# State-space stage, merge and dt of a hybrid decoder block: rooms in another order, dt's chain elsewhere, exponents without a mask product

## The chip, the cores and the metric

The kernel runs on one core of a Trainium2 chip. The metric is the time of one execution in device microseconds (us), as the median of several runs. A profiled execution gives the trace: what each engine did and when, in us from the start of its span. The engines are TensorE (PE, matmuls; PEld is its loading of weights), VectorE (DVE), ScalarE (ACT), GpSimd (POOL) and SyncE (SP), which here issues the transfers between the chip's memory and the working memory (DMA).

## The reference

One layer of a hybrid decoder block on a sequence of 1024 tokens of width 1024, in float32. After a norm, one input projection gives the queries, keys and values of a stick-breaking attention with 16 heads, the z, x, B, C and dt of a Mamba-2 state-space mixer with 32 heads in 4 groups, and two gates per channel. Both branches are projected to the width, gated and summed, and go through an output projection; then come a cross-attention into 256 memory tokens and a feed-forward part. The lines that matter here are those of the mixer:

```
dt = softplus(dt_raw + dt_bias);  a = -exp(a_log)
a_cs = cumsum(dt * a)                       # within each chunk of 128
decay = exp(where(tril, a_cs[l] - a_cs[s], -inf))
cb = einsum('bclgn,bcsgn->bcgls', C, B)
y_diag = einsum('bcgls,bcgels,bcsgep->bclgep', cb, decay, x * dt)
states = einsum('bclgn,bcgel,bclgep->bcgepn', B, exp(a_cs[-1] - a_cs), x * dt)
```

The mask `tril` keeps, in each 128 x 128 square of a chunk, the pairs in which the source is not later than the target.

## The kernel before, in words

Matmuls of float32 values are made as three products of two-part values: a higher part (a copy in the matmul's own format, mostly by ACT, helper line L94) and a lower part (the difference, mostly by DVE, helper line L97). L100, L101 and L102 are these three products. The order of the work on each engine is not written out: a scheduler with a model of the engines sets it when the program is built, from the order in the source, the dependences and the rooms (the named buffers of each pool). Pools are placed one after the other in the working memory, so that a pool's place in the source also decides whose earlier room it takes over, and which earlier work it must wait for.

The stages that matter here, with their times in the trace of before:

- **z stage, to about 270 us.** `token_major` makes a pair of column blocks of v or z from seven (or, with two made early, five) block products of 48 matmuls each, in a scheme that saves one product in eight. Each product's steps split a piece of the weights (L94 by ACT, L97 `zl<-zr,zh` by DVE, three rooms) and make 12 matmuls. The pieces come in by `zr` loads. Sums of products are made in rooms named "zk", six in all (L542, L545, L550).
- **Conv stage, about 270 to 700 us.** x, B and C are made in pairs of row blocks (`winograd_pair`, L218 to L239), convolved on DVE (L602) and transposed. `dt_chain` (L633 to L678) runs inside it, ahead of the seventh pair: it loads the raw dt, laid out as 128 rows of 256, computes softplus by a series (L647 to L660), the sum along each chunk by a scan (L666), and the logarithm of dt (L670), and writes the sums and keys in two parts to the scratch arrays `sum_d` and `key_d` (L674 to L678). `dt_columns`, two pairs later, takes dt and the sums from `dts`.
- **Attention**, to about 1102 us.
- **State-space stage, about 1102 to 1500 us.** 32 chunks (4 groups of 8). `open_four` prepares B, C and cb (L995, L997) for four chunks. `prep` makes the exponents of a chunk as a matmul of two arrays of rows: `keyrows` (keys, and two rows of ones) and `colrows` (a pattern of ones, and the sums), 512 columns at a time (L1021). Ahead of it, a product of the identity and `bar` (L1020) puts the mask, -2^120 above the diagonal, into the same accumulator. ACT takes the exponential (L1022), DVE multiplies by cb (L1023). Then come the states (pst), the outputs (po, and the 16 small matmuls pd, L1073), the norm and the `flip` (four transposes, L1095), and the projection of the branch. Beside the first chunks, `memory` norms and transposes the 256 memory tokens (L1147 to L1154) and the K and V products of the cross-attention are made from them (`mm<-oth,bw` with 256 columns first). Raw weights ("wraw") and split weights ("bw") share the pool "w3".
- **Merge, from about 1500 us.** The attention's output is loaded from `o_d` and split (L1309, "m2" rooms), multiplied by the attention branch's weights (`both`, L1296, one block f of 128 columns ahead), gated and added; the weights of the output projection (`w_mix_out`, L1277) come in meanwhile.

All DMA issues named here stand in SP's one queue, in order.

Of the kernel before, what the change touches and what calls it, by code (L numbers as in the profile page):

```python
# [8 lines left out]
F32 = mybir.dt.float32  # L9
F32R = mybir.dt.float32r  # L10
# [6 lines left out]
P = 128  # L17
# [13 lines left out]
FILL_LEFT, FILL_RIGHT = 96, 224  # L31


@with_exitstack
def hybrid_block(ctx, tc, a, out, dbg=None):
# [44 lines left out]
    u_d = scr("u_d", [4, P, HALF])  # L80

# [167 lines left out]
    with ExitStack() as pa:  # L249
# [214 lines left out]
        with ExitStack() as p1:  # L464
# [24 lines left out]
            def token_major(j, c0, put, i0, early=False):  # L489
# [10 lines left out]
                def times(*args):  # L500
                    for f in product(*args):
                        f()

# [53 lines left out]
            token_major(1, C_Z, put_z, 0, True)  # L557
# [11 lines left out]
        with ExitStack() as p1:  # L569
# [63 lines left out]
            def dt_chain():  # L633
                aneg = mk(cp, [P, 1], F32, "aneg")
                for q in range(4):
                    nc.sync.dma_start(aneg[q * 32:(q + 1) * 32], a["a_log"][0].unsqueeze(1))
                A.activation(aneg, aneg, AF.Exp)

                QT = S // 4
                da, db = [mk(t4, [P, S], F32, "b4") for _ in range(2)]  # L640
                u, e, rc, q_ = [da[:, i * QT:(i + 1) * QT] for i in range(4)]
                keep = db[:, 0:QT]
                dtb = mk(cp, [P, 1], F32, "dtb")
                for q in range(4):
                    nc.sync.dma_start(u[q * 32:(q + 1) * 32], dt_d[:, q * QT:(q + 1) * QT])
                    nc.sync.dma_start(dtb[q * 32:(q + 1) * 32], a["dt_bias"][0].unsqueeze(1))
                V.tensor_scalar(u, u, dtb, None, ALU.add)  # L647
                V.scalar_tensor_tensor(e, u, -1.0, u, ALU.mult, ALU.max)
                A.activation(e, e, AF.Exp, scale=-1.0)

                V.tensor_scalar(rc, e, 2.0, None, ALU.add)
                V.reciprocal(rc, rc)
                V.tensor_tensor(e, e, rc, ALU.mult)
                s2 = rc
                V.tensor_tensor(s2, e, e, ALU.mult)
                V.tensor_scalar(q_, s2, 1.0 / 17, None, ALU.mult)
                for i in range(7, 0, -1):
                    V.scalar_tensor_tensor(q_, q_, 1.0 / (2 * i + 1), s2, ALU.add, ALU.mult)
                V.scalar_tensor_tensor(q_, q_, 1.0, e, ALU.add, ALU.mult)
                V.tensor_scalar(q_, q_, 2.0, None, ALU.mult)  # L660
                dtf, adt, acs = dts[:, 0], e, dts[:, 1]
                V.scalar_tensor_tensor(dtf, u, 0.0, q_, ALU.max, ALU.add)
                V.tensor_scalar(adt, dtf, aneg, -1.0, ALU.mult, ALU.mult)
                G.memset(keep, 1.0)
                G.memset(keep.rearrange("h (c t) -> h c t", t=P)[:, :, 0:1], 0.0)
                V.tensor_tensor_scan(acs, keep, adt, 0.0, ALU.mult, ALU.add)  # L666

                key, ln = db[:, QT:2 * QT], db[:, 2 * QT:3 * QT]
                V.tensor_scalar(key, dtf, 1e-37, None, ALU.max)
                A.activation(ln, key, AF.Ln)  # L670
                V.tensor_tensor(key, ln, acs, ALU.subtract)
                for (src, dst), (hi, lo) in zip(((acs, sum_d), (key, key_d)), ((u, e), (rc, q_))):
                    hi, lo = hi.bitcast(F32R), lo.bitcast(F32R)
                    V.tensor_copy(hi, src)  # L674
                    lo_of(lo, src, hi)
                    for j, t in enumerate((hi, lo)):
                        for q in range(4):
# [1182 lines left out]
```

## Time and profile before

| | us |
|---|---|
| median of three runs (lowest, highest) | 2608.21 (2608.04, 2610.14) |
| the profiled execution | 2607.02 |
| its span | 2605.2 |
| PE busy | 2507.7 (96%) |
| DVE busy | 1826.8 (70%) |
| ACT busy | 1152.4 (44%) |
| POOL busy | 891.3 (34%) |
| mean granted TensorE clock | 0.991 of full speed |

Busy time is the time in which an engine has an instruction in hand. Matmuls are pipelined, so their recorded lengths overlap: 12090 matmuls are recorded. A row of the groups of instructions gives line, engine, operation, out<-in with shapes and count, then the busy time and the mean ns of one, then the idle time ahead of them and what ended it. A row of the waits gives who waited for whom, us in all, times, and the longest.

### The profile page before, as it was taken

How to read it: one execution, taken by the hardware profiler on the slowest of the kernel's cores; microseconds unless marked ns; L12 is line 12 of the kernel's file. 1: busy time of each engine (PE TensorE's matmuls, PEld its weight loads, DVE VectorE, ACT ScalarE, POOL GpSimd, SP SyncE). 2: the span in 40 equal slices, each digit the busy share in tenths (PEclk: the TensorE clock that was granted, in tenths of full speed). 3: DMA queues.
4: the chain of work that ended last, by engine and by line, in shares of the span. 5: the costliest groups of instructions: out<-in, count | busy, mean ns of one | idle time of the engine just before them, and what ended most of it. 6: DMA issues, size and time to landing. Idle time of an engine off the chain costs nothing. (4 is left out here: it accounts for less than half of the span.)

```text
span 2605.2 us, 32757 instructions
## 1 busy us (share of the span) xinstructions
PE 2507.7 (96%) x12090; PEld 2078.6 (80%) x12090; DVE 1826.8 (70%) x2111; ACT 1152.4 (44%) x2053; POOL 891.3 (34%) x686
## 2 busy tenths in 40 slices
PE   8999999999999999979999999999999999999998
PEld 6788787787787778777888878887787888888877
DVE  7675777776689898687788654415549566666997
ACT  6333455554466665455544312314333333334433
POOL 5330544443111111254555231100113333333675
PEclk9999999999999999999999999999999999999999
DMA  6441333333422322255332362221231223224322
GB/s 227 151 138 68 126 122 107 100 105 112 115 77 58 89 68 67 90 166 185 107 92 72 119 201 77 100 86 42 93 121 60 90 73 98 73 89 178 129 97 97
DMA packets 243755, 278.02 MB, mean 107 GB/s; under 512 B 14975, under 2 KB 171272, under 8 KB 243210
## 3 DMA queue, kind: packets, MB, share of 16 engines
q1 hardware_dynamic: 243594, 275.92, 33.4%
q8 instruction: 95, 1.56, 0.2%
q14 instruction: 66, 0.54, 0.1%
HBM read 197.61 MB, written 69.87 MB: 103 GB/s over the span
## 5 line engine op out<-in xcount | busy, mean ns | idle before, releaser
L834 DVE TENSOR_TENSOR_SCAN n<-n,mask 128x128 f32<-128x128 f32 (+7 forms) x128 | 180.2, 1432 | 10.4 <-ACT n L833 7.7
L97 DVE TENSOR_TENSOR sw<-sf,sw 128x512 fp32r<-128x512 f32 x150 | 128.2, 868 | 64.0 <-ACT sw L94 63.6
L194 POOL TENSOR_TENSOR sf<-wr,wr 128x512 f32<-128x512 f32 x38 | 57.1, 1504 | 290.9 <-DMA wr<-in_w_gu_dram 105.7
L853 ACT ACTIVATE wth<-tr,mone 128x512 fp32r<-128x512 f32 x192 | 111.1, 581 | 75.6 <-PE tr L850 74.0
L94 ACT ACTIVATE sw<-sf 128x512 fp32r<-128x512 f32 x150 | 91.8, 626 | 102.2 <-PE mm L220 90.4
L854 DVE SCALAR_TENSOR_TENSOR wtl<-tr,wth 128x512 fp32r<-128x512 f32 x192 | 101.6, 546 | 39.2 <-ACT wth L853 37.8
L97 DVE TENSOR_TENSOR sw<-wr,sw 128x512 fp32r<-128x512 f32 x113 | 107.8, 956 | 30.2 <-ACT sw L94 25.8
L94 ACT ACTIVATE sw<-wr 128x512 fp32r<-128x512 f32 x113 | 71.0, 629 | 127.9 <-PE mm L220 126.7
L220 PE MATMUL mm<-h,sw 128*128 128x512 f32 x320 | 125.0, 392 | 1.8 <-DVE sw L97 1.8
L218 PE MATMUL mm<-h,sw 128*128 128x512 f32 x320 | 122.6, 391 | 3.1 <-ACT h L94 2.3
L219 PE MATMUL mm<-h,sw 128*128 128x512 f32 x320 | 125.3, 391 | 0.0
L100 PE MATMUL mm<-oth,bw 128*128 128x512 f32 (+1 forms) x320 | 122.1, 381 | 0.3 <-ACT a L1130 0.3
L102 PE MATMUL mm<-oth,bw 128*128 128x512 f32 (+1 forms) x320 | 119.0, 372 | 0.3 <-DVE bw L97 0.3
L101 PE MATMUL mm<-otl,bw 128*128 128x512 f32 (+1 forms) x320 | 118.5, 370 | 0.0
L90 POOL TENSOR_SCALAR v<-va 128x512 fp32r<-128x512 f32 x16 | 20.7, 1296 | 279.1 <-PE av L863 148.7
L602 DVE SCALAR_TENSOR_TENSOR b<-b,prmT,b 128x1023 f32<-128x1023 f32 (+2 forms) x72 | 106.0, 1472 | 12.6 <-ACT b L600 12.1
L163 POOL TENSOR_SCALAR rstd<-ms 128x1 f32<-128x1 f32 x82 | 33.1, 404 | 233.5 <-ACT x L1352 112.6
L833 ACT ACTIVATE n<-sc 128x512 f32<-128x512 f32 (+1 forms) x192 | 89.2, 487 | 48.6 <-PE tr L850 23.1
L100 PE MATMUL p<-bw,h 128*128 128x512 f32 x256 | 98.6, 390 | 3.3 <-DVE x L1354 2.4
L97 DVE TENSOR_TENSOR zl<-zr,zh 128x512 fp32r<-128x512 f32 x84 | 72.7, 880 | 40.5 <-ACT zh L94 40.4
L196 POOL TENSOR_TENSOR sf<-wr 128x512 f32<-128x512 f32 x38 | 63.6, 1675 | 108.3 <-DVE sw L97 108.3
L102 PE MATMUL p<-bw,h 128*128 128x512 f32 x256 | 100.5, 393 | 0.1
(595 smaller groups left out, 8266.2 us busy)
## 6 DMA issues: line engine op xcount, KB each, us to landing
wr<-in_w_gu_dram SPq DMA_DIRECT2D x80, 256.0 KB
wr<-in_w_in_dram SPq DMA_DIRECT2D x36, 512.0 KB
zr<-in_w_in_dram SPq DMA_DIRECT2D x32, 512.0 KB
gu_d<-t SPq DMA_DIRECT2D x44, 256.0 KB
wraw<-in_w_in_dram SPq DMA_DIRECT2D x20, 512.0 KB
xs_d<-b SPq DMA_DIRECT2D x32, 256.0 KB
s<-xs_d SPq DMA_DIRECT2D x32, 256.0 KB
s<-zs_d SPq DMA_DIRECT2D x32, 256.0 KB
```

The lines of the kernel that those rows point to most:

```text
L94: A.activation(o, i, AF.Copy)
L97: eng.tensor_tensor(o, i, hi.bitcast(F32), ALU.subtract)
L100: first = T.matmul(ps, sh, mh, start=start, stop=False)
L101: T.matmul(ps, sh, ml, start=False, stop=False)
L102: T.matmul(ps, sl, mh, start=False, stop=stop)
L218: T.matmul(ps, w[0][:, k, :], b[0][:, k, :], start=first and k == 0, stop=False, skip_group_check=True)
L219: T.matmul(ps, w[0][:, k, :], b[1][:, k, :], start=False, stop=False, skip_group_check=True)
L220: T.matmul(ps, w[1][:, k, :], b[0][:, k, :], start=False, stop=last and k == 3, skip_group_check=True)
L602: V.scalar_tensor_tensor(acc[:, sh:], y[:, :S - sh], cw(3 - sh, f), acc[:, sh:], ALU.mult, ALU.add)
L834: V.tensor_tensor_scan(nt[:, 0:L][:, ::-1], nt[:, 0:L][:, ::-1], mask[:, S - L:][:, ::-1], 1.0, ALU.mult, ALU.max)
L853: A.activation(wh[:, t0 * P:], pt[:, t0 * P:], AF.Identity, bias=mone)
L854: V.scalar_tensor_tensor(wl[:, t0 * P:], pt[:, t0 * P:], -1.0, wh[:, t0 * P:].bitcast(F32), ALU.add, ALU.subtract)
```

## The change

Four things change. The mask of the exponents is no longer a product: `colrows` is filled with -2^120 in those rows (times the identity, so that each key row that isn't a head's or a one's picks out one column), `keyrows` holds ones above the diagonal in these rows, and so the one product L1021 also adds a large negative number to most masked places; what is left over is dealt with by a triangle on cb (an `affine_select` on POOL, per four chunks) and by cutting the exponential at 3e38 in the product with cb, which becomes a three-operand instruction. dt's chain becomes a generator whose pieces are issued between the steps of z's first pair; its rooms are four of the six "zk", and dt and its sums go through a new scratch array `dts_d`, from where the conv stage loads them at its start. The raw weights of the state-space stage get a pool of their own. In the merge, the pool of the branch's weights and their load come first in the source, and the loads of the attention's output take turns between two new rooms and four "m2" (six before).

```diff
+BIG, FAR = 3.0e38, -(2.0 ** 120)
...
+    dts_d = scr("dts_d", [2, P, S // 4])
...
+            def dt_chain():
+                QT = S // 4
+                aneg, dtb = [mk(cp, [P, 1], F32, n) for n in ("aneg", "dtb")]
+                rooms = [mk(kp, [P, HALF], F32, "zk") for _ in range(4)]
+                u, e, rc, q_, keep, key, ln, dtf = [t[:, i * QT:(i + 1) * QT] for t in rooms for i in range(2)]
...
+                for j, t in enumerate((dtf, acs)):
+                    nc.sync.dma_start(dts_d[j], t)
...
-            def token_major(j, c0, put, i0, early=False):
+            def token_major(j, c0, put, i0, early=False, beside=()):
+                beside = iter(beside)
...
                     for f in product(*args):
                         f()
+                        next(beside, None)
...
-            token_major(1, C_Z, put_z, 0, True)
+            token_major(1, C_Z, put_z, 0, True, dt_chain())
...
-            def dt_chain():
...
+            for j in range(2):
+                nc.sync.dma_start(dts[:, j], dts_d[j])
             for i, j in enumerate(order):
-                if i == 6:
-                    dt_chain()
...
+        wr = pool(p3, "w3raw", 3)
         wp = pool(p3, "w3", 2)
...
-        identr = mk(ep, [P, P], F32R, "identr")
-        V.tensor_copy(identr, ident)
-        bar = mk(ep, [P, 4, P], F32R, "bar")
-        tri = mk(t4, [P, GH, P], F32, "s4")
-        G.memset(tri, 0.0)
-        G.affine_select(tri, tri, [[0, GH], [1, P]], ALU.is_ge, -(2.0 ** 120), base=0, channel_multiplier=-1)
-        V.tensor_copy(bar, tri[:, 0:4, :])
...
-        for t in colrows + keyrows:
-            G.memset(t.bitcast(F32), 0.0)
         for t in colrows:
+            V.tensor_scalar(t, ident.unsqueeze(1).to_broadcast([P, GH, P]), FAR, None, ALU.mult)
+            for r, n in ((0, GH), (32, GH), (ONES, 2)):
+                V.tensor_scalar(t[:, :, r:r + n], ident[:, r + n:r + n + 1].unsqueeze(1).to_broadcast([P, GH, n]), FAR, None, ALU.mult)
...
+        u = mk(sm, [P, 4, P], F32, "cb")
+        G.memset(u, 1.0)
+        G.affine_select(u, u, [[0, 4], [1, P]], ALU.is_gt, 0.0, base=0, channel_multiplier=-1)
         for t in keyrows:
+            V.tensor_copy(t, u.rearrange("p c i -> p (c i)"))
...
             A.activation(cb, pm, AF.Copy)
+            G.affine_select(cb, cb, [[0, 4], [1, P]], ALU.is_ge, 0.0, base=0, channel_multiplier=-1)
...
-                T.matmul(pe, identr, bar, start=True, stop=False)
-                T.matmul(pe, f4["keys"][:, cs], cr[:, hs, :], start=False, stop=True)
+                T.matmul(pe, f4["keys"][:, cs], cr[:, hs, :], start=True, stop=True)
...
-            V.tensor_tensor(seg, seg, f4["cb"][:, ci, :].unsqueeze(1).to_broadcast([P, GH, P]), ALU.mult)
+            V.scalar_tensor_tensor(seg, seg, BIG, f4["cb"][:, ci, :].unsqueeze(1).to_broadcast([P, GH, P]), ALU.min, ALU.mult)
...
-            xt = mk(wp, [P, D], F32, "wraw", bufs=3)
+            xt = mk(wr, [P, D], F32, "wraw")
...
+        wp = pool(p4, "w4", 1)
+        ol_ = pool(p4, "oload", 2)
         op = pool(p4, "oatt")
-        t2 = pool(p4, "t2m", 6)
-        wp = pool(p4, "w4", 1)
+        t2 = pool(p4, "t2m", 4)
...
-                t = mk(t2, [P, HALF], F32, "m2")
+                t = mk(t2 if k % 2 else ol_, [P, HALF], F32, "m2")
```

The scheduler's order follows from this. At the opening of the state-space stage, PE before; `mm` with 256 columns is memory's K product, `ptr` a flip, `po` and `pst` are outputs and states (the numbers behind a name tell one buffer from another):

```order
L100 MATMUL po_10761<-sth_10478,ch_10142 128x512
L101 MATMUL po_10761<-stl_10479,ch_10142 128x512
L102 MATMUL po_10761<-sth_10478,cl_10143 128x512
L100 MATMUL pst_10843<-s2r_10709,bh_10557 128x512
L1095 MATMUL ptr_10804<-ident_86,s_2148_10505 128x128 x4
L100 MATMUL mm_10251<-oth_10126,bw_10237 128x256
L101 MATMUL mm_10251<-otl_10127,bw_10237 128x256
L102 MATMUL mm_10251<-oth_10126,bw_10237 128x256
```

and PE now, where in the changed file L102 to L104 are the three products, L1079 is pd and L1101 the flip:

```order
L102 MATMUL pst_10726<-s2r_10590,bh_10560 128x512
L1079 MATMUL pd_10517<-s_2077_10184,s_2078_10186 128x96 x7
L1079 MATMUL pd_10517<-s_2077_10184,s_2078_10186 128x64
L103 MATMUL pst_10726<-s2r_10591,bh_10560 128x512
L104 MATMUL pst_10726<-s2r_10590,bl_10561 128x512
L102 MATMUL mm_10258<-oth_10136,bw_10244 128x256
L103 MATMUL mm_10258<-otl_10137,bw_10244 128x256
L104 MATMUL mm_10258<-oth_10136,bw_10244 128x256
```

Before, two flips and several outputs stand ahead of the K product; now no flip does, and the first comes far into K.

SP's queue between the state-space stage and the merge, before (`o_d` is the attention's output, `g_d` the gates):

```order
L1114 DMA wraw_13610<-in_w_br_ssm_dram 128x2x512
L1060 DMA s_2857_13487<-zs_d 128x512
L1060 DMA s_2872_13560<-zs_d 128x512
L1309 DMA m_2903_13857<-o_d 128x512
...
L1321 DMA m_2952_14080<-g_d 128x512
L1319 DMA m_2954_14110<-g_d 128x512
L1296 DMA wraw_13851<-in_w_br_att_dram 128x8x128
L1296 DMA wraw_13936<-in_w_br_att_dram 128x8x128
L1277 DMA wraw_14482<-in_w_mix_out_dram 128x1024
L1321 DMA m_2955_14112<-g_d 128x512
```

and now:

```order
L1066 DMA s_2872_13514<-zs_d 128x512
L1303 DMA wraw_13809<-in_w_br_att_dram 128x8x128
L1316 DMA m_2903_13815<-o_d 128x512
L1316 DMA m_2904_13819<-o_d 128x512
L1316 DMA m_2907_13825<-o_d 128x512
L1316 DMA m_2908_13829<-o_d 128x512
L1316 DMA m_2915_13845<-o_d 128x512
L1316 DMA m_2916_13849<-o_d 128x512
L1303 DMA wraw_13894<-in_w_br_att_dram 128x8x128
L1303 DMA wraw_13963<-in_w_br_att_dram 128x8x128
L1303 DMA wraw_14032<-in_w_br_att_dram 128x8x128
```

The branch's first weights stood behind 16 loads of the attention's output and eleven of gates; now they stand ahead of all of them, and the next three follow the sixth load.

DVE in z's first pair, now; L504 to L516 are pieces of dt's chain, L99 is the lower half of a weight piece, L607 a sum of v:

```order
L99 TENSOR_TENSOR zl_1486<-zr_1457,zh_1485 128x512
L99 TENSOR_TENSOR zl_1526<-zr_1457,zh_1525 128x512
L504 TENSOR_SCALAR zk_1503<-zk_1503,dtb_1502 128x256
L505 SCALAR_TENSOR_TENSOR zk_1503<-zk_1503 128x256
L508 TENSOR_SCALAR zk_1504<-zk_1503 128x256
L509 RECIPROCAL zk_1504<-zk_1504 128x256
L510 TENSOR_TENSOR zk_1503<-zk_1503,zk_1504 128x256
L512 TENSOR_TENSOR zk_1504<-zk_1503 128x256
L513 TENSOR_SCALAR zk_1504<-zk_1504 128x256
L516 SCALAR_TENSOR_TENSOR zk_1504<-zk_1504 128x256
L607 TENSOR_TENSOR zu_561<-zu_561,ma_1193 128x512
```

The chain's first eight instructions stand together between two lower halves; the rest of it is strewn among the halves and sums that follow.

91 lines of the change are left out of this document (45 added, 46 removed).

## The prediction

> **What bounds the kernel now.** I read the page's busy shares first, then stretches, then the waits of TensorE (PE), and last the single instructions at the places that the change touches. The first row is the page's:
>
> ```profile
> PE 2507.7 (96%) x12090; PEld 2078.6 (80%) x12090; DVE 1826.8 (70%) x2111; ACT 1152.4 (44%) x2053; POOL 891.3 (34%) x686
> ```
>
> PE is the bound of the whole: 2605.2 - 2507.7 = 97.5 us idle. What a change is worth is therefore the matmuls that it takes away, and the idle PE time (with the lower granted clock around it) that it closes. Then stretches of the conv stage, of the state-space stage's opening, and one of 100 us of its steady part; columns are the stretch, then busy us of PE, PEld, DVE, ACT and POOL, granted clock, DMA share:
>
> ```profile
> 400.00:450.00 50.00, 45.11 (x190) 36.05 (x189) 45.00 (x56) 28.02 (x40) 21.45 (x13) 0.93 0.30 86
> ```
> ```profile
> 1100.00:1150.00 50.00, 35.22 (x183) 28.43 (x183) 46.82 (x56) 31.44 (x58) 34.50 (x30) 0.90 0.50 150
> 1150.00:1200.00 50.00, 46.67 (x309) 42.14 (x308) 29.17 (x30) 25.70 (x42) 15.31 (x14) 0.98 0.57 172
> ```
> ```profile
> 1300.00:1400.00 100.00, 100.00 (x549) 85.61 (x548) 86.11 (x107) 47.59 (x92) 55.52 (x54) 1.00 0.31 93
> ```
>
> From about 1200 the state-space stage is PE's alone, with VectorE (DVE) next at 86 of 100. Its first 45 us are DVE's: 46.8 of 50, and PE idles 14.8 us. The conv stage has a smaller hole of 4.9 us. PE's waits, one row from each of three stretches (1095 to 1160, 1480 to 1600, 400 to 450):
>
> ```profile
> PE ptr L1095 <- ACT s L1082: 8.6, 2, 4.8
> ```
> ```profile
> PE mm L100 <- ACT both L94: 4.8, 1, 4.8
> ```
> ```profile
> PE mm L218 <- DVE b L237: 2.3, 1, 2.3
> ```
>
> **The mask product (L1020).** It is gone. In two stretches of the listing of that line alone, and in one chunk of the steady part:
>
> ```profile
> 1100.00:1144.00 44.00, 6.89 (x14) 2.94 (x14) 0.91 0.52 158
> 1144.00:1440.00 296.00, 22.14 (x50) 9.49 (x50) 0.99 0.39 119
> ```
> ```profile
> 1302.53 0.48 PE L1020 MATMUL dec<-bar,identr 128*128 128x512 f32 x1
> 1302.84 0.40 PE L1021 MATMUL dec<-colrows,keyrows 128*128 128x512 f32 x1
> 1303.08 0.40 PE L1020 MATMUL dec<-bar,identr 128*128 128x512 f32 x1
> 1303.31 0.40 PE L1021 MATMUL dec<-colrows,keyrows 128*128 128x512 f32 x1
> 1303.54 0.39 PE L100 MATMUL mm<-oth,bw 128*128 128x512 f32 x1
> ```
>
> The recorded lengths (0.40 to 0.48) overlap; what a matmul costs is the step from start to start. The four take 1.01 us from 1302.53 to 1303.54, the first 0.31 behind the small flips, the others 0.23. Two remaining ones would take 0.31 + 0.23 = 0.54, so 0.47 is saved for two, 0.235 each. The 50 behind 1144 lie where PE is the bound: 50 x 0.235 = **11.7 us**. The 14 ahead lie where DVE is, and I count them at nothing; with them it would be 15.0, the upper end. The lower end is about 6, if half is taken back by waits for DVE.
>
> What takes the mask's place lies on the other engines. Prices from the groups of instructions by shape, then the product with cb by itself (shortest, median and longest ns) and in the steady 100 us:
>
> ```profile
> L172 DVE SCALAR_TENSOR_TENSOR x<-x,rstd,g_pre_xa 128x1024 f32<-128x1024 f32 x8 | 10.3, 1284 | 12.9 <-POOL rstd L164 12.9
> L957 POOL TENSOR_SCALAR_AFFINE_SELECT s<-s 128x1024 f32<-128x1024 f32 x1 | 2.7, 2732 | 0.1
> ```
> ```profile
> L1023 DVE TENSOR_TENSOR s<-s,cb x32: 1208/1224/2309, 1111.6 to 1439.8; 128x1024 f32<-128x1024 f32 x32
> ```
> ```profile
> 1300.00:1400.00 100.00, 14.21 (x10) 1.00 0.31 93
> ```
>
> The product with cb becomes a three-operand form. Its row is 1.28 undisturbed, against 1.22 for the median of L1023, so 32 x 0.06 = 1.9 us more of DVE. Ten such products in 100 us mean 10.0 us a chunk, with 8.6 of DVE in it; without two mask products the chunk is 9.5 for PE and 8.7 for DVE: nothing on the path, 1.9 if that cover is gone. Eight triangles on cb on GpSimd (POOL), 128x512 each: by half of L957 some 1.4 us, 11 in all, in a stage where POOL has 44 of 100 free. Each stands between the copy of cb and the first product with it, so it delays one DVE instruction per four chunks; at the stage's opening that is on the path (below), later cb is made chunks ahead.
>
> The Trainium skill, "GPSIMD Engine Reference", section "8. Key points", says that GpSimd and VectorE contend when VectorE's instruction has two SBUF inputs. That speaks against the change, since a triangle would hold up a product, and by it up to 11 us more of DVE time would be spent. The 14.21 us of ten L1023, against a median of 1.22, agree; 8.7 + 0.35 a chunk is still under 9.5, and the sum would stay.
>
> **The opening of the state-space stage.** Here the order of PE changes: memory's K product now stands ahead of the first two flips (L1095).
>
> ```profile
> 1143.42 1.12 PE L1095 MATMUL ptr<-ident,s 128*128 128x128 f32 x4 [4.84 <-ACT s L1082]
> 1144.19 0.56 PE L100 MATMUL mm<-oth,bw 128*128 128x256 f32 x1
> ```
> ```profile
> 1103.82 3.78 DVE L967 CAST colrows<-ident 8x1024 fp32r<-8x1024 f32 x4
> ...
> 1142.11 0.68 DVE L1154 TENSOR_TENSOR otl<-mm,oth 128x512 fp32r<-128x512 f32 x1
> ```
>
> It looks as if the 8.6 us of waiting at the flips (two waits) went away, and I don't count them so. The K product needs the last lower half of memory, DVE's L1154 at 1142.11, and DVE is busy almost without a break to there. With the prices of before, DVE's rows from the set-up to that instruction come to an estimated 34 us before and 31 now: two products with cb and some six halves and sums fewer, against about 4 us of new set-up (two 128x1024 fills, two 128x512 casts, six small ones; a 128x256 scalar operation is 0.28, so about 1.1 for a fill). At the rate at which DVE got through its 34 (39 us) K starts some 4 us sooner. The deferred work (one pd of 16 at about 1.9, eight flips at 1.1 the four, some 0.9 of po and pst) then still has to be done in PE-bound time, some 4 to 5 us. That cancels. What is left as gain is that K and V, long runs of matmuls that wait for little, lie beside DVE's backlog, so the 3.3 us of idle and the clock of 0.98 at 1150 to 1200 may shrink. I take **-3 us**, between -10 (most of the 14.8 idle closes) and +4 (the first cb waits 1.4 for its triangle, and K no sooner).
>
> **The merge.** The attention branch's first weights were issued late:
>
> ```profile
> 1499.36 1.05 SPq L1296 DMA_DIRECT2D wraw<-in_w_br_att_dram  x2
> ```
> ```profile
> 1499.60 0.39 PE L102 MATMUL mm<-oth,bw 128*128 128x512 f32 x1
> 1504.80 0.61 PE L100 MATMUL mm<-oh,both 128*128 128x512 f32 x1 [4.82 <-ACT both L94]
> 1505.21 0.63 PE L101 MATMUL mm<-ol,both 128*128 128x512 f32 x1
> 1505.64 0.63 PE L100 MATMUL mm<-oh,both 128*128 128x512 f32 x1
> ```
>
> Now that load stands ahead of the o loads, which SP issued from 1451, and both its splits stand on DVE ahead of the last sums. The wait of 4.8 goes, and with it the slow start: eight steps at 0.43 in place of 0.23 are 1.6 more. **-6 us**; -3 if the o loads, of which the last two are now issued behind four gate loads, come late by half of that.
>
> The Trainium skill, "TensorE: Matmul & The Clock Gate", section "HAM oscillation — how this bites in real kernels", has the clock fall only behind gaps of more than about 3.4 us. The 4.82 gap agrees. By that rule the gaps of about 2 us in the next part would cost no clock; the granted 0.83 there says otherwise, and by the rule the sum there would be 4.9 at most and not up to 8.
>
> **dt's chain out of the conv stage.** Ten-us stretches, DVE's first and last row of the chain, and two waits there (DVE's and SP's):
>
> ```profile
> 420.00:430.00 10.00, 7.18 (x25) 4.94 (x23) 9.97 (x12) 2.74 (x5) 6.06 (x4) 0.83 0.07 27
> 430.00:440.00 10.00, 7.94 (x31) 6.26 (x32) 9.86 (x14) 5.89 (x10) 3.08 (x2) 0.83 0.25 69
> ```
> ```profile
> 404.90 0.34 DVE L647 TENSOR_SCALAR b<-b,dtb 128x256 f32<-128x256 f32 x1
> ...
> 442.06 0.42 DVE L97 TENSOR_TENSOR b<-b,b 128x256 fp32r<-128x256 f32 x1
> ```
> ```profile
> DVE sw L97 <- DMA b<-dt_d: 4.3, 1, 4.3
> ```
> ```profile
> SPq L191 <- DVE b L674: 19.6, 1, 19.6
> ```
>
> DVE is full from 410 to 440 and the 25 instructions of the chain, about 14 us summed, are between its rows; without them the stretch isn't DVE's. PE loses 2.82 + 2.06 = 4.9 idle there, and 0.17 of some 15 busy us by the clock, 2.6: 7.5 in all. SP's weight loads also no longer stand 19.6 us behind the chain's room. I take **-5 us**, between -8 and 0 (the same waits on the conv's own work).
>
> **The chain in z's first pair.** It comes at about 125 to 160:
>
> ```profile
> 130.00:140.00 10.00, 10.00 (x45) 8.28 (x45) 7.14 (x4) 4.23 (x9) 9.92 (x4) 1.00 0.33 107
> 140.00:150.00 10.00, 9.92 (x44) 7.85 (x43) 7.07 (x11) 4.19 (x8) 0.35 (x1) 1.00 0.83 273
> 150.00:160.00 10.00, 10.00 (x46) 8.29 (x45) 4.52 (x7) 2.53 (x4) 0.00 (x0) 1.00 0.47 149
> ```
>
> Free DVE time there is 2.9 + 2.9 + 5.5 = 11 us of 30 for about 14, part of which falls ahead and behind. Behind the chain's wait for its first exponential (a table load and one ACT instruction) and the reciprocal (1.75 where it was) queue DVE's lower halves of the weights, with three rooms, so PE reaches one late if DVE is away for over about 5 us. Of the chain's DMAs, 18 writes now stand in SP's queue ahead of five weight loads of z's second pair, whose start is five products of 10.9 us (48 steps of 0.227) behind that of the first: nothing. **+1 us**, from 0 to +8.
>
> **Sum.** -11.7 - 3 - 6 - 5 + 1 = -24.7, from the profiled execution's 2607.0 to 2582.3. The median of the runs shown is 1.2 above that execution, so **2583.5**. With the terms' ends partly together, its own range is 2574 to 2592.
>
> **The rivals.**
> *Only the matmuls* (0.22): the stalls move rather than go. For it: DVE stays near 80% in the conv stage even without the chain, and the last o loads now come behind gate loads. Against: the late weight load is plainly the cause of the 4.8. It gives -11.7 + 1, so 2597.5.
> *The opening closes* (0.14): K and V fill the idle PE time while DVE works off its backlog; -10 there and -8 in the conv stage. For it: the flips no longer stand in the way. Against: DVE's work up to K hardly shrinks. -11.7 - 10 - 6 - 8 + 1 = -34.7: 2573.5.
> *z's pair stops for the chain* (0.08): DVE waits in order for dt's load, the exponential and the rooms that the chain's writes hold, and PE with it: 14 + 4.3 = 18 in place of 1. For it: 4.3 of waiting for that load on DVE before. Against: 11 us free in 30. 2600.5.
> *DVE becomes the state-space stage's bound* (0.06), the slower side. Of a chunk's 10.0 us before, 8.6 are DVE's, 1.4 of them the product with cb; once its new form costs over 2.8, DVE alone needs more than 10.0, and each tenth above costs 3.2 us over the 32. At some 4.0, three times the row's 1.28 (half speed for the form, and half as much again beside POOL), 32 x 1.2 = 38 lost, against 13 gained in the other terms, 2633. Against it: the form's row above is 1.28.
>
> **How the numbers follow.** My forecast has 0.50, and is the time given. The range takes in *only the matmuls* and most of the opening: 2570 to 2601. About 0.2% (5 us) is what a measurement of this kernel can tell from no change, so same is 2603 to 2613. Faster takes the forecast, two rivals whole and a quarter of z's (whose time is 2.5 us under the bound): 0.88; same takes the rest of z's, 0.06; slower is DVE's case, 0.06.
>
> **What would show it.** PE's rows 64 fewer, chunks of about 9.5 us in the steady part with DVE near 91 of 100 and no new wait of PE on the product with cb; no wait on `both` at the merge; PE full from 420 to 440 and clock 1.00; PE still full from 120 to 170. The opening is the least sure: PE busy in its first 50 us near 36 to 40. If DVE's product with cb is above 2 us, or PE waits on a lower half in z's pair, the forecast is wrong at that term.

## The result

| | before | after |
|---|---|---|
| median, us (lowest to highest) | 2608.26 (2607.42 to 2610.53) | 2593.61 (2589.49 to 2597.35) |
| profiled execution, us | 2607.02 | 2590.97 |
| its span, us | 2605.2 | 2589.3 |

The ratio is 0.9942, with a 95% interval of 0.9929 to 0.9955: 14.65 us faster by the medians, where 24.7 were forecast. The first row of the page of after, busy us of each engine:

```profile
PE 2491.0 (96%) x12026; PEld 2061.8 (80%) x12026; DVE 1824.0 (70%) x2119; ACT 1149.1 (44%) x2052; POOL 881.1 (34%) x690
```

The 64 mask matmuls are gone (12090 less 12026), and 16.7 us of busy PE; the span lost 15.9, so PE's idle time has hardly changed in all. It has moved. Marks in the two traces, each the start of a first or last matmul (of DVE's last `m<-m,mm` at the merge's end), say where:

| stretch, us | before | after | difference | forecast |
|---|---|---|---|---|
| to the mark in z | 225.9 | 234.3 | +8.4 | +1 |
| the rest of z and conv, to attention's first scores | 449.3 | 440.3 | -9.0 | -5 |
| attention | 426.9 | 423.9 | -3.0 | 0 |
| attention's end to the first K product | 42.1 | 37.2 | -4.9 | |
| first K product to the last flip | 328.2 | 323.7 | -4.5 | |
| these two together | 370.3 | 360.9 | -9.4 | -14.7 |
| last flip to the end of the merge | 121.5 | 116.9 | -4.6 | -6 |
| the rest | 1011.3 | 1013.0 | +1.7 | 0 |
| sum | 2605.2 | 2589.3 | -15.9 | -24.7 |

The mark in z is the last matmul `ma<-zh,b21h`, in the third of the seven products of z's second pair. z's last matmul ends some 44.4 us behind it (270.2 before, 278.7 after), in every run, so that differences are those of z's end. Where "z ends" or "the conv stage takes" stands below, and in the expectations, this mark is meant.

**z.** PE waited once, for the sum that frees its next accumulator room (waits of PE, 100 to 150; the matmul behind it; 10 us with the granted clock, which is the 0.69):

```profile
PE ma L290 <- DVE zu L607: 6.3, 1, 6.3
```
```profile
145.31 0.77 PE L290 MATMUL ma<-zh,t2h 128*128 128x512 f32 x1 [6.32 <-DVE zu L607]
```
```profile
140.00:150.00 10.00, 4.69 (x11) 3.75 (x12) 9.35 (x18) 4.38 (x8) 0.02 (x1) 0.69 0.30 69
```

DVE's timeline says why that sum came late. First the sum before (there it is L553) and the first matmul into the room that it frees, then after:

```profile
137.28 0.69 DVE L553 TENSOR_TENSOR zu<-zu,ma 128x512 f32<-128x512 f32 x1 [1.67 <-PE ma L290]
```
```profile
139.12 0.39 PE L288 MATMUL ma<-zh,t2h 128*128 128x512 f32 x1
```
```profile
135.24 2.52 DVE L504 TENSOR_SCALAR zk<-zk,dtb 128x256 f32<-128x256 f32 x1
137.79 2.51 DVE L505 SCALAR_TENSOR_TENSOR zk<-zk 128x256 f32<-128x256 f32 x1
...
141.11 1.75 DVE L509 RECIPROCAL zk<-zk 128x256 f32<-128x256 f32 x1
...
144.48 0.68 DVE L607 TENSOR_TENSOR zu<-zu,ma 128x512 f32<-128x512 f32 x1
```

Eight pieces of the chain stand ahead of the first sum, which came 7.2 us later. L504 and L505 took 2.5 us each; in before the same two instructions, at 404.90 and 407.56, took 0.34 and 0.41. Beside them GpSimd ran these sums of weights:

```profile
134.72 2.84 POOL L575 TENSOR_TENSOR zr<-zr,zr 128x1024 f32<-128x1024 f32 x1
137.51 0.09 POOL L502 MEMSET zk<- 128x2 f32 x1
137.65 2.37 POOL L583 TENSOR_TENSOR zr<-zr,zr 128x1024 f32<-128x1024 f32 x1
```

L504 ended at 137.76 and L575 at 137.56; L505 at 140.30 and L583 at 140.02. So each instruction of DVE's seems to have waited until GpSimd's was through, though its row books the wait as busy time. The rest of the trace bears this out: of 134 lower halves of 128x512 that began inside a GpSimd instruction with over 0.6 us left to run, 116 took over 1.3 times the 0.68 us of those that began beside an idle GpSimd, and in the median they ended 0.55 us behind GpSimd's. The other 18 were not held up.

**Conv.** The same stretches as in the prediction:

```profile
400.00:450.00 50.00, 47.80 (x215) 39.38 (x214) 36.29 (x34) 24.32 (x37) 25.89 (x14) 1.00 0.38 116
420.00:430.00 10.00, 10.00 (x46) 8.29 (x45) 9.28 (x9) 3.67 (x5) 4.90 (x3) 1.00 0.51 157
430.00:440.00 10.00, 7.80 (x39) 6.26 (x38) 5.70 (x6) 6.14 (x10) 5.74 (x4) 1.00 0.18 46
```

The hole at 420 has closed and the clock is full; a gap of 2.2 us, for GpSimd's part of the convolution, is left at 430.

**State-space stage.** Stretches of its opening, then PE's longest waits there, then two rows of DVE's set-up (the fills and the last copies of the row tiles):

```profile
1100.00:1150.00 50.00, 35.97 (x201) 29.84 (x200) 39.64 (x49) 28.40 (x50) 23.29 (x24) 0.80 0.51 156
1150.00:1200.00 50.00, 47.46 (x283) 40.80 (x282) 36.96 (x41) 27.49 (x47) 17.74 (x17) 1.00 0.63 202
```
```profile
PE dec L1027 <- DMA colrows<-sum_d: 4.3, 1, 4.3
PE pst L102 <- ACT state L1049: 2.7, 1, 2.7
PE pd L1079 <- DVE s L1082: 2.7, 1, 2.7
```
```profile
1098.33 1.28 DVE L965 TENSOR_SCALAR colrows<-ident 128x1024 fp32r<-128x1024 f32 x2
...
1102.27 4.02 DVE L969 CAST colrows<-ident 8x1024 fp32r<-8x1024 f32 x4
```

The wait at the flips (8.6) is gone, and three others stand in its place: the first exponent waits for its rows, whose two loads SP issued at 1103.3 and 1104.0, while DVE's four small copies (to 1106.3) were still under way, and which landed at 1108.7 and 1108.9. DVE has less to do, 39.6 of 50 in place of 46.8, and PE idles as long as before, at a clock of 0.80 in place of 0.90. Then the steady part: 100 us, the product with cb and the triangle (count, shortest, median and longest ns), and PE's waits from 1160 to 1470:

```profile
1300.00:1400.00 100.00, 98.82 (x541) 83.85 (x540) 87.95 (x110) 48.72 (x95) 58.03 (x60) 1.00 0.29 89
```
```profile
L1029 DVE SCALAR_TENSOR_TENSOR s<-s,cb x32: 1206/1222/2308, 1119.6 to 1429.0; 128x1024 f32<-128x1024 f32 x32
```
```profile
L1004 POOL TENSOR_SCALAR_AFFINE_SELECT cb<-cb x8: 634/636/822, 1102.2 to 1396.8; 128x512 f32<-128x512 f32 x8
```
```profile
PE mm L103 <- DVE bw L99: 1.1, 2, 0.8
PE po L103 <- DVE stl L99: 0.7, 1, 0.7
PE dec L1027 <- ACT cb L1003: 0.7, 2, 0.4
```

The product in its three-operand form costs what the two-operand one did (1222 ns against 1224), and the triangle 0.64 us against the 1.4 assumed. PE is idle for 1.2 of 100 us, in many small waits, where it was full before.

**Merge.** PE's waits from 1470 to 1600, and SP's issues:

```profile
PE mm L102 <- DVE a L1138: 0.9, 2, 0.5
PE p L102 <- DVE m L1333: 0.9, 1, 0.9
```
```profile
1441.83 0.38 SPq L1303 DMA_DIRECT2D wraw<-in_w_br_att_dram  x1
...
1461.69 6.16 SPq L1316 DMA_DIRECT2D m<-o_d  x8
```

The wait of 4.8 on `both` is gone; its weights are issued 58 us earlier, 45 us earlier as seen from the last flip.

### The profile page after: what moved, and what is told of

It reads as the page before. It is cut to its first block, busy times and chain, and to the rows that moved or that the text cites. A ratio compares the mean times of both kernels' runs of the same rounds, so it can differ in the third digit from the quotient of the medians.

```text
span 2589.3 us, 32651 instructions
## 1 busy us (share of the span) xinstructions
PE 2491.0 (96%) x12026; PEld 2061.8 (80%) x12026; DVE 1824.0 (70%) x2119; ACT 1149.1 (44%) x2052; POOL 881.1 (34%) x690
## 5 line engine op out<-in xcount | busy, mean ns | idle before, releaser
L99 DVE TENSOR_TENSOR sw<-sf,sw 128x512 fp32r<-128x512 f32 x150 | 128.9, 872 | 65.1 <-ACT sw L96 64.5
L99 DVE TENSOR_TENSOR sw<-wr,sw 128x512 fp32r<-128x512 f32 x113 | 107.0, 950 | 31.6 <-ACT sw L96 31.5
L102 PE MATMUL mm<-oth,bw 128*128 128x512 f32 (+1 forms) x320 | 122.3, 382 | 2.1 <-DVE a L1138 1.5
L104 PE MATMUL mm<-oth,bw 128*128 128x512 f32 (+1 forms) x320 | 119.2, 372 | 0.6 <-DVE bw L1125 0.4
L165 POOL TENSOR_SCALAR rstd<-ms 128x1 f32<-128x1 f32 x82 | 27.7, 338 | 239.3 <-ACT x L1359 101.5
L102 PE MATMUL p<-bw,h 128*128 128x512 f32 x256 | 98.9, 391 | 3.3 <-DVE x L1361 2.3
L104 PE MATMUL p<-bw,h 128*128 128x512 f32 x256 | 100.1, 392 | 0.0
L103 PE MATMUL p<-bw,h 128*128 128x512 f32 x256 | 99.8, 390 | 0.0
```

The source lines that it names most:

```text
L99: eng.tensor_tensor(o, i, hi.bitcast(F32), ALU.subtract)
L102: first = T.matmul(ps, sh, mh, start=start, stop=False)
L103: T.matmul(ps, sh, ml, start=False, stop=False)
L104: T.matmul(ps, sl, mh, start=False, stop=stop)
```

## The experiments

Ratios are to the kernel before on the same chip, with 95% intervals. "Stage" is a stretch of the table above.

| kernel | median, us | ratio |
|---|---|---|
| after | 2593.61 | 0.9942 (0.9929 to 0.9955) |
| without dt's move | 2589.56 | 0.9924 (0.9909 to 0.9939) |
| chain in z's second pair | 2586.70 | 0.9904 (0.9888 to 0.9921) |
| the same, measured again | 2584.44 | 0.9920 (0.9906 to 0.9933) |
| chain 8 steps later | 2593.49 | 0.9947 (0.9933 to 0.9961) |
| chain 12 steps later | 2591.17 | 0.9944 (0.9930 to 0.9958) |
| mask's part alone | 2602.49 | 0.9978 (0.9968 to 0.9987) |
| without the mask's part | 2602.19 | 0.9984 (0.9974 to 0.9995) |
| without the raw weights' pool | 2603.13 | 0.9978 (0.9966 to 0.9989) |
| merge's part alone | 2610.33 | 1.0012 (1.0001 to 1.0022) |
| merge's part and the pool | 2597.05 | 0.9959 (0.9940 to 0.9977) |
| set-up on GpSimd | 2590.20 | 0.9939 (0.9921 to 0.9957) |
| second row tile copied | 2589.40 | 0.9938 (0.9922 to 0.9953) |

**dt's chain: is its new place worth it?** All of after but the chain's move:

```diff
-            token_major(1, C_Z, put_z, 0, True, dt_chain())
+            token_major(1, C_Z, put_z, 0, True)
...
+                if i == 6:
+                    dt_chain()
```

> All of the change but the move of dt's chain, which stays in the conv stage. In the trace of the change, z's first pair ends 8.4 us later than before and the attention starts 0.6 us earlier, so the conv stage has given 9.0. Theory: both belong to the chain's move, and they cancel: 2594 +/- 3, PE full from 120 to 170 us, and the holes of PE at 420 to 440 are there again. Rival: the conv stage's gain comes from the scheduler's new order and not from the chain: then the 8.4 go and the 9.0 stay, 2585.

z ends at 226.0 again, and the conv stage takes 447.9: the chain is what closes its hole. PE's waits from 265 to 700, and the stretch at 420, are back:

```profile
PE mm L219 <- ACT b L229: 4.1, 2, 2.4
PE mm L219 <- DVE b L238: 2.9, 3, 2.2
PE mm L219 <- ACT b L233: 1.9, 2, 1.5
```
```profile
420.00:430.00 10.00, 7.12 (x24) 5.09 (x23) 9.96 (x11) 2.75 (x5) 6.23 (x4) 0.83 0.01 5
```

Over all kernels profiled, the conv stage took 439.8 to 442.8 us with the chain moved and 445.9 to 449.6 with it there: some 7 us. Yet the kernel is 4 us faster by the medians without the move (the intervals overlap): what the move wins there, it loses in z. By the two traces z gives 8.3 back and conv takes 7.6; the state-space stage is 2.5 shorter without the move (358.5 against 361.0), and for that no cause is shown. The time lies halfway between the two that were expected.

**The chain beside z's second pair:**

```diff
-            token_major(1, C_Z, put_z, 0, True, dt_chain())
-            token_major(2, C_Z + 2 * HALF, put_z, 2)
+            token_major(1, C_Z, put_z, 0, True)
+            token_major(2, C_Z + 2 * HALF, put_z, 2, False, chain([None] * 4, dt_chain()))
```

> The change, with dt's chain beside z's second pair from its second product on (about 205 us) and not beside the first pair. DVE is busy there 5 of 10 us and GpSimd does nothing. Theory: PE waited 6.3 us in the first pair since the chain's first eight instructions (two of them 2.5 us each beside GpSimd's work on the weights) kept a sum of v, which frees TensorE's accumulators, waiting; in the second pair nothing of that is near, so 8 us come back: 2585.5, no wait of PE over 1 us between 120 and 265. Rival: the chain's in-order waits (dt's load, the exponential, the rooms) stop PE wherever it stands: 2594, with a wait of some 6 us between 205 and 250.

As the theory has it: z ends at 225.5, the conv stage takes 442.8, and PE has no wait at all from 120 to 265. The time is the best of all kernels here, so it was measured once more:

> The kernel after with dt's chain beside z's second pair once more, in more rounds: its first time came from four runs, 2580.9 to 2589.0. Theory (the place of the chain is worth the 6.3 us of PE's wait, of which some come back later): 2586 to 2588, at least 5 us under the kernel after. Rival (the four runs were low, and it stands where the kernel without the chain's move and the one with the copied row tile stand): 2589 to 2590, 3 to 4 us under the kernel after.

2584.44, 9 us under after by the medians and some 6 by the ratios. The first interval lies wholly below that of after, the second overlaps it at the edge (0.9933 against 0.9929). Against the kernel without dt's move the gain is 3 to 5 us by the medians and 1 to 5 by the ratios, and the intervals overlap: that this place beats the old one is likely, not shown. Why the second pair bears the chain I read from the trace alone: DVE's pieces lie at 193 to 218, and GpSimd is idle for 16 of these 25 us in one piece. Two of the chain's instructions that met GpSimd there were held up as well (1.41 and 2.31 us where 0.29 is usual), and no wait of PE came of it.

```profile
194.68 2.40 POOL L576 TENSOR_TENSOR zr<-zr,zr 128x1024 f32<-128x1024 f32 x1 [3.16 <-DVE zl L100]
213.05 2.67 POOL L584 TENSOR_TENSOR zr<-zr,zr 128x1024 f32<-128x1024 f32 x1 [15.97 <-DVE zl L100]
```

**What is late in the first pair?** Two kernels begin the chain eight and twelve steps later in it (the expectations say products, but a step makes 12 matmuls, and four steps are a product of 48); in the first the early pieces still stand ahead of the last sums of v on DVE, in the second they stand behind them.

```diff
-            token_major(1, C_Z, put_z, 0, True, dt_chain())
+            token_major(1, C_Z, put_z, 0, True, chain([None] * 8, dt_chain()))
```

(and `[None] * 12`).

> The kernel after with dt's chain begun eight products later in z's first pair. Its first eight pieces still stand ahead of VectorE's last sums of v, its second half lies later. Theory (the wait is for the bank of sums that the last sums of v set free, and only the pieces ahead of those count): PE waits on that sum again, 4 to 6.5 us, the z stage ends at 232 to 235, and the kernel is as after, 2592 to 2595. Rival (VectorE is short of time over the whole first pair, so that thinning the chain helps): the wait shrinks to under 3 us, stage end at 229 or sooner, 2589 or less.

> The same, begun twelve products later: still in z's first pair, but the chain's first piece now stands behind the last sums of v. Theory (the bank): no wait of PE on that sum, the z stage ends at 226 to 227.5 as before, and the kernel is as with the chain in the second pair, 2586 to 2589. Rival (VectorE's time in the first pair): the lower halves of the weights come late instead, PE waits 3 us or more on them between 140 and 190, stage end 229 or more, 2590 or more.

The first did what the theory says: the same wait of 6.3, z's end at 233.8, and after's time. The second fits neither: z's end and the time are the rival's, the wait is not. The wait on v's sum is gone, the lower halves are not late, and PE waits for a sum further on, again one that frees an accumulator room (waits of PE, 120 to 265):

```profile
PE ma L291 <- DVE zk L605: 4.8, 2, 3.7
```

z ends at 232.5. DVE and GpSimd ahead of that wait:

```profile
183.79 2.50 DVE L513 TENSOR_TENSOR zk<-zk 128x256 f32<-128x256 f32 x1
186.33 2.37 DVE L514 TENSOR_SCALAR zk<-zk 128x256 f32<-128x256 f32 x1
```
```profile
183.50 2.51 POOL L572 TENSOR_TENSOR zr<-zr,zr 128x1024 f32<-128x1024 f32 x1 [3.43 <-DVE zl L100]
186.09 2.45 POOL L574 TENSOR_TENSOR zr<-zr,zr 128x1024 f32<-128x1024 f32 x1
```

In after the same two pieces took 0.42 and 0.29. They end at 186.29 and 188.70, GpSimd's at 186.01 and 188.54. So the theory was too narrow. It is not one room: by these two runs the chain's pieces, several of them stretched beside GpSimd, make late whichever sum of products comes next.

**The mask's part alone**, in the kernel before:

> The kernel before with the mask product alone replaced (triangle on cb, three-operand product). Theory: 11.7 us from 50 matmuls at 0.235, less some 3 of new small waits of PE on DVE and ACT: 2599, with about 9.5 us a chunk in the steady part. Rival: with PE at 9.5 a chunk and DVE at 8.7, DVE or the small waits take half or more of it: 2603 or more.

```diff
-                T.matmul(pe, identr, bar, start=True, stop=False)
-                T.matmul(pe, f4["keys"][:, cs], cr[:, hs, :], start=False, stop=True)
+                T.matmul(pe, f4["keys"][:, cs], cr[:, hs, :], start=True, stop=True)
```

(with all the rows of the diff on `colrows`, `keyrows`, cb and its product). The medians differ by 6.7, and the time lies nearer to the rival's. From the first K product to the last flip it gains 7.1, but the opening is 2.9 longer, since the set-up on DVE now makes the first exponent wait:

```profile
PE dec L1020 <- DVE colrows L962: 4.8, 1, 4.8
PE pd L1072 <- DVE s L1075: 3.8, 2, 3.0
```

**And its complement**, after with the mask product, its tile and the two-operand product put back:

> The kernel after with the mask product, the mask tile and the two-operand product with cb put back, all other parts as in after. Theory from the run of the mask's part alone (-6.7): the part is worth about 7 us, half of what its matmuls take, since the opening waits for DVE and its rows either way and small waits appear in the steady part: 2600, between 2598 and 2602. Rival (the sum of the forecast holds once the other parts are in, since K and V then cover the opening): 11.7 slower than after, 2605.

2602.19, by the median at the edge of what the theory gave; but before ran faster on that chip (2606.75), and by the ratios the part is worth 0.0042 of 2608, 11 us. In the traces the state-space stage takes 372.2 us without the part and 361.0 with it. So the rival is nearer: in the company of the other parts the matmuls bring nearly their full 11.7. Between the two kernels with and without it but without dt's move (0.9959 and 0.9924) it is 9. Each of the three is uncertain by 3 to 6 us; that the part is worth more beside the pool is likely, and no more.

**The raw weights' own pool**, after without it:

```diff
-        wr = pool(p3, "w3raw", 3)
...
-            raw = mk(wr, [P, 2, HALF], F32, "wraw")
+            raw = mk(wp, [P, 2, HALF], F32, "wraw", bufs=3)
```

> The change without the pool of its own for the raw weights of the state-space stage. Theory: that pool lets memory's rows and the first K weights (1.5 MB) be issued ahead of the first rows of sums; the first exponents then waited 4.3 us for these rows and the clock fell to 0.65: without it that wait goes, and K starts as late as the weights come: 2590 to 2594. Rival: the pool is what brings K forward by 5 us against the attention's end (37 us in place of 42); without it K is late again: 2597 or more.

The pool is worth 9.4 us by the ratios, in a place that neither expectation named. The opening took 37.1 us, as in after; the stretch from the last flip to the merge's end took 125.2 in place of 116.9. SP issued all but two of the loads of the attention's output only after the stage's last matmul (1488.4), and PE waited for them:

```profile
1443.75 1.05 SPq L1315 DMA_DIRECT2D m<-o_d  x2
...
1488.45 2.71 SPq L1315 DMA_DIRECT2D m<-o_d  x6
```
```profile
PE mm L102 <- ACT oh L96: 4.5, 3, 1.9
PE mm L104 <- DVE both L99: 2.4, 1, 2.4
```

**The merge's part with and without that pool**, both in the kernel before:

```diff
+        wp = pool(p4, "w4", 1)
+        ol_ = pool(p4, "oload", 2)
         op = pool(p4, "oatt")
-        t2 = pool(p4, "t2m", 6)
-        wp = pool(p4, "w4", 1)
+        t2 = pool(p4, "t2m", 4)
...
-                t = mk(t2, [P, HALF], F32, "m2")
+                t = mk(t2 if k % 2 else ol_, [P, HALF], F32, "m2")
```

> The kernel before with the merge's part alone (the branch weights' pool first, the o loads in a pool of their own for even rows), without the raw weights' own pool in the state-space stage. Theory, from the run without that pool: the new order of the merge's pools puts the first o loads on rooms that the state-space stage still holds, and only the raw weights' own pool makes these rooms free in time. So the wait on both (4.8 us) goes, but the o loads are issued some 40 us later than in the kernel after, and the merge stage takes 97 to 98 us as there: about 2608 + 8.7 - 4.8 - 1.6 = 2610, between 2606 and 2614. Rival (the late o loads in that run came from the other parts' schedule, and the merge's part needs no pool): the forecast's -6 alone, 2602.

> The kernel before with the raw weights' own pool and the merge's part, both, and nothing else. Theory (the two are one change): the o loads are early, the wait on both is gone, the merge stage takes about 87.5 us and starts 3 us sooner behind the last flips: the forecast's -6, so 2602, between 2599 and 2605. Rival (both parts only move the stall to the o loads): no change, 2607 to 2610.

The first came out as the theory has it: the merge's part alone makes the kernel slower, if anything. The wait on `both` doesn't go but halves, to 2.4 us, and all but two of the first loads of the attention's output are issued from 1500 on. With the pool the two bring 9.7 us by the medians, more than the 6 expected. The stretch from the last flip to the merge's end is 123.9 us in the one and 116.4 in the other. The state-space stage is 3.7 us shorter with the pool as well: K starts 33.5 us behind attention's end in place of 41.8, and 4.5 of these 8.2 are given back before the last flip. The pool by itself was not run, so how much of this needs the merge's part is open.

**Does VectorE's backlog set the opening?** Two kernels take work from DVE ahead of K, both with the chain in z's second pair. One moves the set-up to GpSimd:

```diff
-            V.tensor_scalar(t, ident.unsqueeze(1).to_broadcast([P, GH, P]), FAR, None, ALU.mult)
+            G.tensor_scalar(t, ident.unsqueeze(1).to_broadcast([P, GH, P]), FAR, None, ALU.mult)
```

(and so for the small fills, the 8x1024 copies and the casts of `keyrows`).

> The kernel after with dt's chain beside z's second pair, and beside it the set-up of the exponents' rows and keys (two fills 128x1024, six small ones, four 8x1024 copies, two 128x512 casts) on GpSimd in place of VectorE, where GpSimd has gaps of 6 us. It takes about 7.4 us of VectorE from 1098 to 1106. Theory (VectorE's backlog sets when K starts): K starts 4 to 6 us sooner behind attention's end (31 to 33 in place of 37 us), and the kernel is 3 to 5 us faster than with the chain's place alone: 2582 to 2584. Rival one (the opening is bound by transfers and the chain of waits from sum_d's row on, not by VectorE): K within 1 us of 37, 2586 to 2587. Rival two (GpSimd is later with the set-up than VectorE was): the first exponent waits longer than 4.3 us, K later, 2588 or more.

The second rival came true: GpSimd was late. Its fills took 2.8 us each where DVE's took 0.64, and behind its last copies stood the small instructions of memory's norm, so that the norm's product on DVE, and with it K, came late: 44 us behind attention's end. The kernel is 3.5 to 6 us slower by the medians than with the chain's place alone.

```profile
1091.03 2.78 POOL L966 TENSOR_SCALAR colrows<-ident 128x1024 fp32r<-128x1024 f32 x1 [1.80 <-DVE wtl L862]
...
1109.07 3.47 POOL L970 CAST colrows<-ident 8x1024 fp32r<-8x1024 f32 x2
1112.62 1.09 POOL L167 TENSOR_TENSOR rstd<-rstd,mhalf 128x1 f32<-128x1 f32 x2
```

The other makes the second row tile by one copy of the first:

```diff
-        for t in colrows:
+        for t in colrows[:1]:
...
+        V.tensor_copy(colrows[1], colrows[0].bitcast(F32))
```

> The chain beside z's second pair, and the second of the two row tiles made by one copy 128x1024 of the first, in place of its own fill (0.64 us), three small fills (0.33) and two copies 8x1024 (2.0): VectorE has some 3.0 - 1.2 = 1.8 us less ahead of K. Theory (VectorE's backlog sets when K starts): K about 33.5 to 34 us behind attention's end in place of 35.5, and the kernel 1 to 2 us faster than with the chain's place alone, 2585 to 2586. Rival (transfers and waits from the rows of sum_d on set it, and VectorE has gaps of 2 us there): K within 0.5 us of 35.5, 2587.

PE's wait for the first exponent fell from 5.5 us to 1.8, and K came 34.8 us behind attention's end, where the same kernel without the copy had 35.5 and 37.2 in its two profiled executions. No time came of it: 2589.4, by the medians 3 to 5 us slower than with the chain's place alone, whose second interval overlaps this one. What was won was lost later, from 1200 to 1250 (first this kernel, then the one with the chain's place alone; the first number behind the length is PE's busy time):

```profile
1200.00:1250.00 50.00, 45.53 (x228) 36.60 (x227) 39.42 (x44) 28.50 (x57) 28.91 (x28) 0.97 0.45 140
```
```profile
1200.00:1250.00 50.00, 48.53 (x270) 40.98 (x269) 41.24 (x47) 32.36 (x63) 32.41 (x31) 1.00 0.47 149
```

So less work for DVE ahead of K is no gain in itself. What sets the length of the opening and of the 60 us behind it is left open: not DVE's set-up alone, and no single wait.

## Why the prediction was right and wrong

The direction, the order of size and the range were right; the time was 10 us too low. That it wasn't further off is in part luck: z, the state-space stage, the merge and the rest came out 15.8 us above their terms, and conv and attention 7.0 below theirs. By its own steps:

- **The mask product and the opening, -11.7 and -3.** The two stretches gained 9.4 in place of 14.7. The prices were right or too high (the product with cb 1222 ns, the triangle 0.64 us, 64 rows fewer). The term that failed is the opening's -3: the idle time didn't shrink, it found other waits (4.3 for the rows of the sums), and that K and V lie beside DVE's backlog won nothing. The deferral, "that cancels", fits the traces: K 4.9 us sooner, and from K on 4.5 gained where 11.7 of matmuls went. That leaves 7.2: by the prediction's estimate some 4.5 of it is the deferred work, which leaves some 2.7 for small new waits; the steady part shows 1.2 of them in 100 us. I had put these waits into the lower bound alone.
- **The merge, -6.** It gained 4.6, and the wait on `both` went. But the reason was half of it. I costed the order of the loads, and not the raw weights' own pool, to which I gave no price at all. Without it the merge's part gains nothing (2610.33), since its rooms come free only after the stage.
- **The conv stage, -5.** It gained 9.0 in this pair of traces and 7 over all of them. The mechanism was right, the term too small: the hole of 20 us alone had been priced at 7.5, and only 5 of it was taken. The three rows of waits without the move sum to 8.9, and 2.5 of that is left with it; all rows from 265 to 700 went from 15.3 to 9.6.
- **z's first pair, +1.** This is the step that failed: +8.4. I added the chain's 14 us at the durations it had in the conv stage against 11 us of free DVE time, and took the three rooms of the lower halves as the cover, some 5 us. The cover that ended first was the accumulator room, freed by a sum that in before ended at 137.97, 1.2 us ahead of the first matmul into that room (139.12). So 6.3 us of waiting came of a delay of 7.2, and some 2 more of the clock's fall to 0.69 behind it. And the durations were not those of the conv stage: two pieces took 2.5 us each in place of 0.3 to 0.4, which makes 4.3 of the 7.2. The 25 pieces sum to 15.5 us, not far from the 14; the sum of the pieces was not at fault, but which of them stood ahead of the accumulator's sum. By these rows I estimate that without the two long ones the sum would still have come some 2.9 us late. The row quoted in the prediction for 130 to 140 has GpSimd busy for 9.92 of 10 us; I read only DVE's column of it.
- **The rivals.** *z's pair stops for the chain* was the nearest to what happened there, with 18 us priced where 7 came, and for another reason: not dt's load, and only 0.5 us of it the exponential. *Only the matmuls*, at 2597.5, is 4 us off the result and also has z at +1 and the stalls unmoved, so it is right for the opening and wrong for conv and merge. *DVE becomes the bound* fell with the price of 1222 ns.
- **Its signs.** PE was full from 420 to 430 but not to 440, nor from 120 to 170; the opening's 35.97 is at the edge of the 36 to 40 given, and DVE's 87.95 below the 91.
- **What no step had:** attention, with the same code, took 3.0 us less. Two profiled executions of one and the same kernel (the chain in z's second pair) had 429.4 and 424.9 there, so the 3.0 are no effect that these traces can show. The same two differ by 2.0 in the state-space stage and 2.2 in the merge, so smaller differences between single traces say little.

In the prediction I weighed the Trainium skill's "GPSIMD Engine Reference" (section "8. Key points") for the triangles alone. The rule that bears on the chain is told at length in its page "SBUF — State Buffer", section "SBUF: two separate sides": the port pair that GpSimd and VectorE share is an exclusive lock for VectorE's instructions with two inputs there or in a two-port mode, held for a whole instruction, and the loser blocks. The traces agree: four of the chain's instructions, two of them with a single tensor as input, ended 0.16 to 0.28 us behind a GpSimd instruction of 2.4 to 2.8 us that had started first.

## What to carry to other kernels

Before work is moved under another engine's cover, look at what stands behind it in the queue, and take the nearest deadline there: here an accumulator room with 1.2 us to spare, not the weights' rooms with 5. Take the durations from rows with the same neighbours: an instruction of 0.3 us on VectorE can take 2.5 us beside GpSimd's sums, and the busy column of GpSimd at the new place says so beforehand. And a pool moved in the source is a change of its own: it decided when a load of the next stage was issued, and without it the new order of the loads gained nothing.

## What the runs showed of the hardware

The length of a VectorE row seems to include its wait for GpSimd: a 128x256 scalar operation of 0.3 us is recorded as up to 2.5 us of busy time, so a busy share near 10 of 10 (9.67 from 130 to 140 in after) isn't all work. GpSimd took 2.8 us for a fill of 128x1024 for which VectorE took 0.64.

The granted clock fell to 0.69 in the 10 us with a gap of 6.3 us. With a single gap of 2.2 us it went either way. In before it was 0.66 in the 5 us behind the first of the gaps at 420 to 440; there matmuls went from steps of 0.23 to steps of 0.43, ahead of the next gap (0.7 us, to 430.1):

```profile
425.07 0.50 PE L218 MATMUL mm<-t4h,sw 128*128 128x512 f32 x1 [2.26 <-DVE b L237]
...
427.10 0.63 PE L219 MATMUL mm<-t4l,sw 128*128 128x512 f32 x1
```
```profile
425.00:430.00 5.00, 4.36 (x12) 2.94 (x12) 4.97 (x8) 2.10 (x4) 2.17 (x2) 0.66 0.00 0
```

In after, the gap at 430 to 440 is as long, and the clock stayed at 1.00:

```profile
435.86 1.09 PE L646 MATMUL tr<-ident,b 128*128 128x128 f32 x8 [2.20 <-POOL b L658]
```

So neither the length of the longest gap nor a sum of gaps tells these two apart, and what does is open.
